# S5 state parts, sigmoids and latent-key scaling re-placed around two attention blocks

## The chip, the cores and the metric

One Trainium2 chip; the kernel runs on one core. The metric is the device time of one execution in microseconds (us), the median over runs. The engines are called PE (TensorE: matmuls and transposes), DVE (VectorE), ACT (ScalarE), POOL (GpSimd) and SP (SyncE, which here only issues DMAs). Each works through its own instructions in the order in which the program wrote them.

## The reference, cut to what matters

Two layers over 256 latent and 256 context tokens of width 1024. A layer is a half-step SwiGLU, a token mixer with three head groups side by side, and a second half-step SwiGLU. The change lies inside the mixer.

```
def token_mixers(zx, zc, need_ctx_out, ...):        # need_ctx_out: layer 0 only
    a_x = na_attention(rms_norm(heads(qa_x)), rms_norm(heads(ka_x)), va_x, ka_ch, va_ch, na_rpb)
    kb, vb = mla_keys_values(ckv, kr, ...)          # latent attention: low-rank keys and values
    qb_x = rope_tail(mla_queries(cq_x, ...), row, col)
    kb_x = rope_tail(kb_x, row, col)
    b_x = blocked_joint_attention(qb_x, kb_x, vb_x, kb_c, vb_c, MLA_QK ** -0.5)
    s_x, s_c = s5_mixer(u_x, u_c, ...)              # bidirectional complex scan, GELU, GLU
...
def mla_keys_values(ckv, kr, g_ckv, w_ukv, g_k):
    kv = (rms_norm(ckv, g_ckv) @ w_ukv).reshape(B, N, MLA_HEADS, MLA_NOPE + MLA_V_DIM)
    k = rms_norm(concatenate([k_nope, broadcast(kr)], axis=-1), g_k)
...
def readout(ys, u):
    a, g = split(gelu(ys[0] + ys[1] + d_skip * u) @ w_glu + b_glu, 2)
    return a * sigmoid(g)
```

## The kernel before, in words

The order of work is written out by hand: `tc.manual_schedule()` keeps the order of the Python code on every engine. Float32 products of the big projections are done as three matmuls (`mm3`, lines 291 to 293) on weights split into a high part (ACT, line 251) and a rest (line 252: DVE, and for the mixer's weights POOL for the second half); `take` splits the next weight unit ahead.

`mixers` handles one layer's token mixer in this order.

- Five projections by `group`: `cq`, `ckv`, `qa`, `ka`, `va`, each in two halves of weights. After every second `mm3`, `step` pops one entry of the list `self.q` or advances the background generator by one `yield`. The generator is `s5_mix`: in two half-groups (`hg`) it makes the scan of the S5 states on DVE (lines 1075, 1076), multiplies the real and the imaginary part back (`H[0]` and `H[1]`, lines 1084 to 1089) and multiplies both with the output matrices on PE (lines 1099, 1105, result `py`). The transposes of the window attention's queries and keys (`tr`) wait in `self.q` behind seven `None`.
- Up-projections of the latent attention: a list `seq` of token tiles, first the queries, then the four key tiles, each with a head (matmul and eviction), a stat (sum of squares and `rstd`, whose power runs on POOL, line 1140) and a tail. The queries' tail scales and rotates (`rope`); the keys' tail `ktail` scales the 64 plain columns on DVE (line 1359) and the 32 rotated ones on POOL (line 1360).
- The S5 gate: eight `mm3` (`wg`) into four PSUM banks `pg`, the six transposes of the latent queries into `mqT` (line 1123, evictions 1127 and 1131), the sum for the last key tile, the sigmoids (line 1387), the gate's product (line 1391) and its split (lines 1393, 1394).
- `attention`: 36 jobs in layer 0, 24 in layer 1, one per head and block of 128 queries, the window heads first. A job's scores (lines 1468 and 1473, or 1477) go to one of the four PSUM banks that `pg` also uses; maximum on DVE (1480), exponential on ACT (1484), scaling by 1/sum on DVE (1491) one turn later, transposes (1500) three turns later, products with the values (1520) after that. At turn 4 `k_cols` transposes all latent keys, 24 transposes, into `mkT`.

Of the kernel before, what the change touches and what calls it, by code (L numbers as in the profile page):

```python
# [10 lines left out]
F32 = mybir.dt.float32  # L11
F32R = mybir.dt.float32r
AF = mybir.ActivationFunctionType
OP = mybir.AluOpType
# [53 lines left out]
def bc(ap, shape):  # L68
    return ap.to_broadcast(shape)
# [24 lines left out]
class Net:  # L94
# [915 lines left out]
    def s5_mix(self, l, uT, yT):  # L1010
        nc = self.nc
        V, P, S = nc.vector, nc.gpsimd, nc.scalar
        with lines(self.tc, name=f"s5{l}", bufs=1, side="right") as sp:
            Ys = sp.tile([128, 8, 128], F32, name="Ys")
            for hg in range(2):
# [31 lines left out]
                for d in range(2):  # L1047
                    for pr in range(4):
                        for o in range(2):
                            for hf in range(2):  # L1050
# [3 lines left out]
                                q = (d * 4 + pr) * 64  # L1054
# [27 lines left out]
                for o, (x, y, op) in enumerate(((hr, hi, OP.subtract), (hi, hr, OP.add))):  # L1082
                    ua, ub = (ta, tb) if o == 0 else (tc2, td)
                    V.tensor_tensor(v4(ua), v4(x), Ec, op=OP.mult)
                    V.tensor_tensor(v4(ub), v4(y), Es, op=OP.mult)
                    a_, b_ = v4(ua), v4(ub)
                    V.tensor_tensor(H[o][:, 0, :, 1:64], a_[:, 0, :, 0:63], b_[:, 0, :, 0:63], op=op)
                    V.tensor_tensor(H[o][:, 1, :, 30::-1], a_[:, 1, :, 0:31], b_[:, 1, :, 0:31], op=op)
                    V.tensor_tensor(H[o][:, 1, :, 63:31:-1], a_[:, 1, :, 31:63], b_[:, 1, :, 31:63], op=op)
                    yield  # L1090
                for _ in range(4):
                    yield
                py = self.tp()
# [88 lines left out]
    def mixers(self, l, pu, nxt):  # L1182
        nc, I = self.nc, self.I
        V, P, S = nc.vector, nc.gpsimd, nc.scalar
        need = l == 0
        qt_ = [0, 1, 2, 3] if need else [2, 3]
# [3 lines left out]
        mp = pool(es, "mixa")  # L1190
        gb = mp.tile([128, 2, 32], F32, name="gb")
# [16 lines left out]
        def lowrank(z, n, kr=False):  # L1208
            def f(t):
                sq = np_.tile([128, 384], F32, name="sq")  # L1210
                ss = np_.tile([128, 1], F32, name="ss1", bufs=2)
                S.activation(sq[:, 0:n], z[:, t, 0:n], AF.Square, accum_out=ss)
                if kr:
                    S.activation(sq[:, 256:288], z[:, t, 256:288], AF.Square, accum_out=krs[:, t:t + 1])
                self.rstd(np_, ss, 1, n)
                V.tensor_scalar(z[:, t, 0:n], z[:, t, 0:n], ss, None, op0=OP.mult)

            return f
# [9 lines left out]
                    V.tensor_tensor(CG[:, i, 2 + t].rearrange("p (a b c) -> p a b c", a=2, b=2)[:, :, b, :],  # L1228
                                    kc[:, 2 + t].rearrange("p (a b c) -> p a b c", a=2, b=2)[:, :, b, :], g4[:, :, 1 - b, :], op=OP.mult)

        def rope(pl, x, t, i, nh):

            if t < 2:
                V.tensor_tensor(x, x, bc(gb[:, i, :].unsqueeze(1), [128, nh, 32]), op=OP.mult)
                return
            tm = pl.tile([128, nh, 32], F32, name="tm", bufs=2)
            q4 = lambda a: a.rearrange("p h (a b c) -> p h a b c", a=2, b=2)
            sg = CG[:, i, t].rearrange("p (a b c) -> p a b c", a=2, b=2)
            for b in range(2):
                for a in range(2):  # L1240
                    P.tensor_tensor(q4(tm)[:, :, a, b, :], q4(x)[:, :, a, 1 - b, :], bc(sg[:, a, b, :].unsqueeze(1), [128, nh, 8]), op=OP.mult)
            P.tensor_tensor(x, x, bc(CG[:, i, t - 2, :].unsqueeze(1), [128, nh, 32]), op=OP.mult)
            P.tensor_tensor(x, x, tm, op=OP.add)

        def kv(t):
            lowrank(zk, 256, True)(t)
            if t:
                rope(np_, zk[:, t - 1, 256:288].unsqueeze(1), t - 1, 1, 1)

        self.group("ckv", l, 288, al, lambda t: zk[:, t], kv)  # L1250
        rope(np_, zk[:, 3, 256:288].unsqueeze(1), 3, 1, 1)
        for qi, name in enumerate(("qa", "ka")):
            tiles = al if qi else qt_
            qn = np_.tile([128, 4, 384], F32, name="qn", bufs=2)

            def norm(t, qn=qn):
                sq = np_.tile([128, 384], F32, name="sq")
                S.activation(sq, qn[:, t], AF.Square)
                ss = np_.tile([128, 6], F32, name="ss", bufs=2)
                V.tensor_reduce(ss, sq.rearrange("p (h d) -> p h d", h=6), axis=AX, op=OP.add)  # L1260
                self.rstd(np_, ss, 6, 64)
                qv = qn[:, t].rearrange("p (h d) -> p h d", h=6)
                V.tensor_tensor(qv, qv, bc(ss.unsqueeze(2), [128, 6, 64]), op=OP.mult)

            self.group(name, l, 384, tiles, lambda t: qn[:, t], norm)

            def tr(j, qi=qi, tiles=tiles, qn=qn):
                self.transp(nq[qi][:, j, 128 * tiles[0]:], lambda t: qn[:, t, 128 * j:128 * j + 128], 128, tiles, self.kg[l][:, 0:1] if qi else None)

            self.q += [None] * 7 + [(lambda j=j, tr=tr: tr(j)) for j in range(3)]  # L1270
        self.group("va", l, 384, al, lambda t: nv[:, t])
        self.flush()

# [38 lines left out]
        qs, kn = {}, {}  # L1312
        new = lambda: lp.tile([128, 6, 96], F32, name="qn", bufs=4)

        ss = {}

        def stat(key, sq, extra=None):

            ss[key] = lp.tile([128, 6], F32, name="ss6", bufs=4)
            V.tensor_reduce(ss[key], sq, axis=AX, op=OP.add)  # L1320
            if extra is not None:
                V.tensor_scalar(ss[key], ss[key], extra, None, op0=OP.add)
            self.rstd(lp, ss[key], 6, 96)
# [33 lines left out]
        def ktail(t):  # L1357
            r = bc(ss["k", t].unsqueeze(2), [128, 6, 64])
            V.tensor_tensor(kn[t][:, :, 0:64], kn[t][:, :, 0:64], r, op=OP.mult)
            P.tensor_tensor(kn[t][:, :, 64:96], bc(zk[:, t, 256:288].unsqueeze(1), [128, 6, 32]), r[:, :, 0:32], op=OP.mult)  # L1360

        seq = [(qhead, qstat, qtail, t) for t in [2, 3] + qt_[:-2]]
        nqs = len(seq)
        seq += [(khead, kstat, ktail, t) for t in al]
        for i, s_ in enumerate(seq):
            if i == nqs:
                wk = self.take("ukv", (l,), True)[:, :, 0:1536].rearrange("p s (k n) -> p s k n", k=2)
            s_[0](s_[3])
            if i == nqs + 0:
                pass  # L1370
            for j in (1, 2):
                if i >= j:
                    seq[i - j][j](seq[i - j][3])
            if i - nqs - 1 in (0, 1):
                self.window(bias, i - nqs - 1)
# [4 lines left out]
            for k in range(2):  # L1380
                self.mm3(pg[n][:, c], (wg[:, 0, k, n * 128:n * 128 + 128], wg[:, 1, k, n * 128:n * 128 + 128]), (yh[:, 0, k, c], yh[:, 1, k, c]), k == 0, k == 1)
        eg = [zq.rearrange("p t n -> p (t n)")[:, T * n:T * n + T] for n in range(2)]
        for j in range(6):
            self.transp(mq[0][:, j, 128 * qt_[0]:], lambda t: qs[t][:, j, :], 96, qt_, eng="act" if j % 2 else "dve")
        seq[-1][1](seq[-1][3])
        for n in range(2):
            S.activation(eg[n][:, c], pg[2 + n][:, c], AF.Sigmoid, bias=self.smT[l][:, 98 + n:99 + n])
        seq[-2][2](seq[-2][3])
        seq[-1][2](seq[-1][3])
        for n in range(2):  # L1390
            V.scalar_tensor_tensor(eg[n][:, c], pg[n][:, c], self.smT[l][:, 96 + n:97 + n], eg[n][:, c], op0=OP.add, op1=OP.mult)
        for n in range(2):
            S.activation(xn[:, 0, 6 + n, c], eg[n][:, c], AF.Copy)
            (V,P)[n].tensor_tensor(xn[:, 1, 6 + n, c], eg[n][:, c], xn[:, 0, 6 + n, c].bitcast(F32), op=OP.subtract)
        esl.close()
        esr.close()

        def k_cols():
            for j in range(6):
                self.transp(mq[1][:, j, :], lambda t: kn[t][:, j, :], 96, al, self.kg[l][0:96, 1:2], eng="act" if j % 2 else "dve")  # L1400

        self.attention(l, need, nq, nv, mq, mv, bias, xn, k_cols)
# [38 lines left out]
    def attention(self, l, need, nq, nv, mq, mv, bias, ox, k_cols):  # L1441
        nc = self.nc
        V, P, S = nc.vector, nc.gpsimd, nc.scalar
        mm = nc.tensor.matmul
        with lines(self.tc, name=f"att{l}", bufs=1) as ap:
# [83 lines left out]
            for i in range(len(jobs) + LAG):  # L1529
                if i < len(jobs):  # L1530
                    scores(jobs[i])
                if 0 < i <= len(jobs):
                    scale(jobs[i - 1])
                if i >= LAG:
                    transposes(jobs[i - LAG])
                if i == 4:
                    k_cols()
                if i == 6:
                    self.ahead()
                for a in old.pop(0):  # L1540
                    pv(*a)
                old.append(pend[:])
                pend.clear()
# [48 lines left out]
```

## Time and profile before

| | us |
|---|---|
| median of 3 runs | 1966.84 (1964.74 to 1967.74) |
| the profiled execution, its own time | 1965.27 |
| its span, first to last instruction | 1963.5 |
| PE busy | 1906.2 (97%) |
| DVE, ACT, POOL busy | 912.7, 676.5, 559.3 |
| mean granted clock of PE, share of full speed | 0.983 |

PE is busy for 97% of the span, so time can only come out of its few waits and of stretches in which its clock is granted at half. The mixer's part before the feed-forward blocks lies at about 470 to 700 us (layer 0) and 1540 to 1745 us (layer 1).

### The profile page before, as it was taken

What the parts mean: (1) busy time and instruction counts of PE and PEld (TensorE: products, weight loads), DVE (VectorE), ACT (ScalarE), POOL (GpSimd) and SP (SyncE); (2) the same over time, 40 slices, a digit from 0 to 9 for tenths busy, and PEclk for the clock granted to TensorE, in tenths of its full rate; (3) what the DMA queues carried; (4) which work ended last, traced back from release to release, by engine and by line L of the source; (5) the groups of instructions that cost most, each with busy time, mean ns of one, the idle gap of its engine ahead of it and who ended that gap; (6) DMA issues with size and microseconds to landing.
All of it is one profiled execution on the core that took longest, in us unless ns stands there. A gap on an engine that the chain in (4) does not pass through costs nothing.

```text
span 1963.5 us, 28025 instructions
## 1 busy us (share of the span) xinstructions
PE 1906.2 (97%) x11345; PEld 1560.8 (79%) x11345; DVE 912.7 (46%) x1628; ACT 676.5 (34%) x1120; POOL 559.3 (28%) x637
## 2 busy tenths in 40 slices
PE   7999999999999999999999999999999888999999
PEld 4777777788895687788888877777888778579999
DVE  6453233247556835233232554423424745655555
ACT  4421222234444634212222342122223434545443
POOL 2137461124443032101101314745212435131000
PEclk9999999999997999999999999999999999799999
DMA  9656566524440024532322455646523443036563
GB/s 309 178 167 198 175 203 215 162 97 129 145 133 22 1 86 149 172 109 86 107 86 86 129 171 169 208 158 206 167 88 100 141 161 105 22 125 215 177 194 108
DMA packets 364101, 277.76 MB, mean 141 GB/s; under 512 B 29854, under 2 KB 355812, under 8 KB 363972
## 3 DMA queue, kind: packets, MB, share of 16 engines
q1 hardware_dynamic: 361008, 268.44, 43.8%
q0 software_dynamic: 1888, 7.31, 1.0%
q8 instruction: 89, 1.46, 0.3%
q10 hardware_dynamic: 1076, 0.22, 0.1%
q14 instruction: 40, 0.33, 0.1%
HBM read 263.39 MB, written 12.55 MB: 141 GB/s over the span
## 4 chain that ended last, share of the span: by engine, by line
PE 87%; DVE 5%; DMA 2%; POOL 2%; ACT 2%; issue 1%; SPq 1%; DVEq 0%; ACTq 0%; POOLq 0%
PE acc L291 25%; PE acc L292 24%; PE acc L293 24%; PE acc L1468 3%; PE b L467 3%; PE t L1500 1%; PE t L1520 1%; PE acc L1473 1%; DVE xm L562 1%; PE t L1105 1%; DVE xn L572 1%; PE acc L1477 1%; DVE spl L252 1%; POOL sqs L523 1%; PE t L1123 1%
## 5 line engine op out<-in xcount | busy, mean ns | idle before, releaser
L291 PE MATMUL acc<-xn,spl 128*128 128x512 f32 (+1 forms) x1664 | 597.1, 359 | 4.7 <-DVE mv L1348 2.7
L292 PE MATMUL acc<-xn,spl 128*128 128x512 f32 (+1 forms) x1664 | 590.2, 355 | 1.6 <-DVE xn L396 0.2
L293 PE MATMUL acc<-xn,spl 128*128 128x512 f32 (+1 forms) x1664 | 586.7, 353 | 0.1
L252 DVE TENSOR_TENSOR spl<-raw,spl 128x1024 fp32r<-128x1024 f32 (+2 forms) x312 | 393.2, 1296 | 274.4 <-ACT spl L251 272.3
L251 ACT ACTIVATE spl<-raw 128x1024 fp32r<-128x1024 f32 (+3 forms) x344 | 324.0, 990 | 307.5 <-PE acc L293 165.5
L291 PEld LDWEIGHTS acc<-xn,spl 128*128 128x128 f32 x1664 | 315.0, 189 | 67.3 <-issue 21.1
L292 PEld LDWEIGHTS acc<-xn,spl 128*128 128x128 f32 x1664 | 315.3, 189 | 46.5 <-DVE xn L570 4.0
L293 PEld LDWEIGHTS acc<-xn,spl 128*128 128x128 f32 x1664 | 315.1, 189 | 44.4 <-DVE spl L252 0.9
L672 POOL TENSOR_TENSOR hid<-hv,hid 128x512 fp32r<-128x512 f32 (+1 forms) x88 | 101.8, 1156 | 853.4 <-ACT hid L671 853.4
L291 PE MATMUL acc<-hid,spl 128*128 128x512 f32 (+1 forms) x740 | 265.2, 358 | 0.0
L292 PE MATMUL acc<-hid,spl 128*128 128x512 f32 (+1 forms) x740 | 262.0, 354 | 0.0
L293 PE MATMUL acc<-hid,spl 128*128 128x512 f32 (+1 forms) x740 | 261.8, 354 | 0.0
L669 DVE TENSOR_TENSOR hv<-sl,acc 128x512 f32<-128x512 f32 (+1 forms) x88 | 54.6, 621 | 360.1 <-PE acc L293 348.1
L729 DVE SCALAR_TENSOR_TENSOR h<-acc,mod,h 128x256 f32<-128x256 f32 x192 | 85.0, 479 | 210.3 <-PE acc L293 210.3
L671 ACT ACTIVATE hid<-hv 128x512 fp32r<-128x512 f32 (+1 forms) x88 | 50.9, 579 | 382.3 <-DVE hv L669 382.3
L291 PEld LDWEIGHTS acc<-hid,spl 128*128 128x128 f32 x740 | 139.8, 189 | 25.1 <-issue 6.4
L293 PEld LDWEIGHTS acc<-hid,spl 128*128 128x128 f32 x740 | 139.9, 189 | 19.7
L292 PEld LDWEIGHTS acc<-hid,spl 128*128 128x128 f32 x740 | 140.0, 189 | 18.6
L252 POOL TENSOR_TENSOR spl<-raw,spl 128x768 fp32r<-128x768 f32 (+3 forms) x32 | 65.0, 2030 | 214.4 <-ACT spl L251 204.0
L291 PE MATMUL acc<-spl,xn 128*128 128x384 f32 (+1 forms) x322 | 108.7, 338 | 0.0
L292 PE MATMUL acc<-spl,xn 128*128 128x384 f32 (+1 forms) x322 | 105.1, 326 | 1.1 <-DVE spl L252 1.1
L293 PE MATMUL acc<-spl,xn 128*128 128x384 f32 (+1 forms) x322 | 104.6, 325 | 0.0
(360 smaller groups left out, 1993.4 us busy)
## 6 DMA issues: line engine op xcount, KB each, us to landing
raw<-in_ffn_w_gu SPq DMA_DIRECT2D x176, 512.0 KB
raw<-in_w_mod SPq DMA_DIRECT2D x64, 1024.0 KB
raw<-in_ffn_w_down SPq DMA_DIRECT2D x32, 1024.0 KB
raw<-in_ffn_w_down SPq DMA_DIRECT2D x16, 768.0 KB
raw<-in_w_in SPq DMA_DIRECT2D x16, 768.0 KB
pmod<-in_w_mod SPq DMA_DIRECT2D x8, 1024.0 KB
raw<-in_w_out SPq DMA_DIRECT2D x8, 1024.0 KB
cld<-CL POOLq DMA_DIRECT2D x8, 576.0 KB, 4.1
```

What stands on the lines that cost most here:

```text
L251: nc.scalar.activation(s[:, 0, a:b], raw[:, a:b], AF.Copy)
L252: (nc.gpsimd if mix and b == n else nc.vector).tensor_tensor(s[:, 1, a:b], raw[:, a:b], s[:, 0, a:b].bitcast(F32), op=OP.subtract)
L291: mm(out, sl[0], sr[0], start=start, stop=False)
L292: mm(out, sl[0], sr[1], start=False, stop=False)
L293: mm(out, sl[1], sr[0], start=False, stop=stop)
L467: nc.tensor.matmul(p[32 * j:32 * j + 32, 0:256], self.cs[:, k, 6 - 2 * w:38 - 2 * w], raw[:, k, :], start=(a == 0 and w == 0), stop=(a == ...
L523: nc.gpsimd.tensor_tensor(self.sq_sum[:, c], self.sq_sum[:, c], s[:, c], op=OP.add)
L669: nc.vector.tensor_tensor(hv[:, c], sl[:, c], pu[:, c], op=OP.mult)
L671: nc.scalar.activation(hd[:, 0, c], hv[:, c], AF.Copy)
L672: nc.gpsimd.tensor_tensor(hd[:, 1, c], hv[:, c], hd[:, 0, c].bitcast(F32), op=OP.subtract)
L729: self.nc.vector.scalar_tensor_tensor(self.h[:, n, c], ps[:, c], self.mod[l][:, gate, n, s:s + 1], self.h[:, n, c], op0=OP.mult, op1=OP.add)
L1468: mm(s, q[:, 256 + 128 * t:384 + 128 * t], k, start=True, stop=h >= 6)
```

## The change

Four edits.

1. In `s5_mix` both parts `H[0]` and `H[1]` are made in one turn of the generator. Before, one turn lay between them; five turns pass behind the second part as before, so the second part and the products `py` stand one turn, that is two `mm3`, earlier.
2. `rope` for the shared rotated key columns writes into a tile of its own, `kr`, and its four small POOL products become two of twice the width.
3. The transposes of the window queries and keys wait behind nine `None` instead of seven.
4. In front of the attention: the keys' tails leave the list; the sigmoids stand before the query transposes, of which three come before and three after the gate's product; the four `ktail` go into turns 2 to 5 of the attention, the key transposes into turns 6 and 7 (twelve each), and `self.ahead()` (the split of the next weights) from turn 6 to turn 8. The keys' sums get a tile `ssk` that outlives the pool.

```diff
                     V.tensor_tensor(H[o][:, 1, :, 63:31:-1], ...)
-                    yield
-                for _ in range(4):
+                for _ in range(5):
                     yield
...
+        kr = mp.tile([128, 4, 32], F32, name="kr")
+        def rope(pl, x, t, i, nh, to=None):
+            to = x if to is None else to
...
             for b in range(2):
-                for a in range(2):
-                    P.tensor_tensor(q4(tm)[:, :, a, b, :], q4(x)[:, :, a, 1 - b, :], bc(sg[:, a, b, :]...), op=OP.mult)
+                P.tensor_tensor(q4(tm)[:, :, :, b, :], q4(x)[:, :, :, 1 - b, :], bc(sg[:, :, b, :]...), op=OP.mult)
...
-            self.q += [None] * 7 + [(lambda j=j, tr=tr: tr(j)) for j in range(3)]
+            self.q += [None] * 9 + [(lambda j=j, tr=tr: tr(j)) for j in range(3)]
...
-                if i >= j:
+                if i >= j and (j == 1 or i - j < nqs):
                     seq[i - j][j](seq[i - j][3])
...
-        for j in range(6):
-            self.transp(mq[0][:, j, ...], ..., 96, qt_, eng="act" if j % 2 else "dve")
         seq[-1][1](seq[-1][3])
         for n in range(2):
             S.activation(eg[n][:, c], pg[2 + n][:, c], AF.Sigmoid, ...)
-        seq[-2][2](seq[-2][3])
-        seq[-1][2](seq[-1][3])
+        for j in range(3):
+            self.transp(mq[0][:, j, ...], ..., 96, qt_, eng="act" if j == 2 else "dve")
...
+        for j in range(3, 6):
+            self.transp(mq[0][:, j, ...], ..., 96, qt_, eng="act" if j % 2 else "dve")
...
-        def k_cols():
-            for j in range(6):
+        def k_cols(n):
+            if n < 4:
+                ktail(n)
+                return
+            for j in range(3 * n - 12, 3 * n - 9):
...
-                if i == 4:
-                    k_cols()
-                if i == 6:
+                if 1 < i < 8:
+                    k_cols(i - 2)
+                if i == 8:
                     self.ahead()
```

On DVE in layer 1, second half-group of the S5 part, before: the last product of the real part, the norms of two query tiles (`qn`), the split of the next weights (line 252), and then the imaginary part (the second `H`).

```order
L1089 TENSOR_TENSOR H_12574<-ab 128x4x32
L1156 COPY qn<-acc 128x384
L1260 TENSOR_REDUCE ss<-sq 128x6
L1139 TENSOR_SCALAR ss<-ss 128x6
L1263 TENSOR_TENSOR qn<-qn,ss 128x384
...
L252 TENSOR_TENSOR spl<-raw,spl 128x768
L1084 TENSOR_TENSOR ab<-si,E 128x512
L1085 TENSOR_TENSOR ab<-sr,E 128x512
L1087 TENSOR_TENSOR H_12575<-ab 128x4x63
```

The same place in the change, from the four products in front of the scan (`ab`) on; one split (line 252) now stands behind those products instead of before them.

```order
L1067 TENSOR_TENSOR ab<-t,E 128x512
L252 TENSOR_TENSOR spl<-raw,spl 128x768
...
L1089 TENSOR_TENSOR H_12555<-ab 128x4x32
L1084 TENSOR_TENSOR ab<-si,E 128x512
L1085 TENSOR_TENSOR ab<-sr,E 128x512
L1087 TENSOR_TENSOR H_12556<-ab 128x4x63
...
L1155 COPY qn<-acc 128x384
L1261 TENSOR_REDUCE ss<-sq 128x6
```

The second part has moved in front of both norms and of the split that followed them.

On ACT in layer 1, ahead of the attention, before: the evictions of three query transposes, the squares of the last key tile, the load of the sigmoid's table and the sigmoids (into `zq`).

```order
L1127 ACTIVATE mqT<-b 96x256
L1127 ACTIVATE mqT<-t 96x256
L1127 ACTIVATE mqT<-b 96x256
L1354 ACTIVATE sq_13266<-kn 128x6x64
L1387 ACT_TABLE_LOAD
L1387 ACTIVATE zq<-acc,smT_91 128x256 x2
L1393 ACTIVATE xn<-zq 128x256 x2
```

And in the change:

```order
L1356 ACTIVATE sq_13219<-kn 128x6x64
L1387 ACT_TABLE_LOAD
L1387 ACTIVATE zq<-acc,smT_91 128x256 x2
L1126 ACTIVATE mqT<-t 96x256
L1393 ACTIVATE xn<-zq 128x256 x2
L1126 ACTIVATE mqT<-t 96x256
L1126 ACTIVATE mqT<-b 96x256
```

The sigmoids no longer stand behind any eviction of a transpose.

On DVE at the same place of layer 1, before: the sums and powers of the last two key tiles, their scalings (line 1359), and between them the evictions of three query transposes.

```order
L1359 TENSOR_TENSOR kn<-kn,ss_13141 128x6x64
L1348 COPY kn<-acc 128x3x64
L1348 COPY mv<-acc 128x192
...
L1359 TENSOR_TENSOR kn<-kn,ss_13176 128x6x64
L1131 COPY mqT<-t 96x256 x3
...
L1359 TENSOR_TENSOR kn<-kn,ss_13205 128x6x64
L1359 TENSOR_TENSOR kn<-kn,ss_13268 128x6x64
L1391 SCALAR_TENSOR_TENSOR zq<-acc,smT_91,zq 128x256 x2
```

And in the change:

```order
L1350 COPY kn<-acc 128x3x64
L1350 COPY mv<-acc 128x192
...
L1138 TENSOR_SCALAR ssk<-ssk 128x6
L1130 COPY mqT<-t 96x256
L1130 COPY mqT<-b 96x256
L1391 SCALAR_TENSOR_TENSOR zq<-acc,smT_91,zq 128x256 x2
L1394 TENSOR_TENSOR xn<-zq,xn 128x256
L1130 COPY mqT<-t 96x256
```

No scaling of keys, which waits for a power on POOL, is left in front of the evictions; the four scalings follow within the first attention jobs.

## Rows read from the trace of the kernel before

**Rows 1.** Stretches around layer 0's first attention jobs; columns in the first line.

```profile
core 0: us, PE busy (x) PEld busy (x) DVE busy (x) ACT busy (x) POOL busy (x), PEclk, DMA share, GB/s
599.00:604.00 5.00, 2.66 (x4) 0.99 (x4) 3.40 (x7) 3.27 (x5) 2.82 (x3) 0.70 0.00 0
614.00:619.00 5.00, 5.00 (x20) 3.76 (x19) 3.29 (x8) 2.28 (x7) 0.00 (x0) 0.50 0.00 0
619.00:624.00 5.00, 5.00 (x28) 4.15 (x27) 2.63 (x4) 2.05 (x3) 0.00 (x0) 0.76 0.00 0
634.00:639.00 5.00, 5.00 (x28) 3.02 (x27) 4.54 (x12) 2.76 (x10) 0.00 (x0) 1.00 0.42 147
```

**Rows 2.** Stretches of layer 1's mixer, the same columns.

```profile
1632.00:1636.00 4.00, 2.60 (x15) 2.31 (x16) 2.91 (x3) 2.60 (x4) 0.77 (x2) 1.00 0.16 43
1664.00:1668.00 4.00, 1.10 (x5) 0.65 (x4) 1.95 (x4) 0.86 (x3) 4.00 (x5) 0.74 0.00 0
1688.00:1692.00 4.00, 4.00 (x25) 3.36 (x23) 2.90 (x5) 2.29 (x5) 0.00 (x0) 0.77 0.00 0
```

**Rows 3.** PE's waits in layer 0's mixer: total us, times, longest us.

```profile
PE acc L1468 <- ACT zq L1387: 3.1, 1, 3.1
PE acc L291 <- DVE mv L1348: 1.5, 1, 1.5
PE t L1105 <- DVE H L1087: 1.3, 1, 1.3
PE b L1123 <- DVE qn L1263: 1.0, 1, 1.0
PE acc L292 <- DVE spl L252: 0.7, 2, 0.4
```

**Rows 4.** PE's waits in layer 1's mixer, the same columns.

```profile
PE t L1105 <- DVE H L1087: 7.0, 1, 7.0
...
PE acc L1468 <- ACT zq L1387: 2.7, 1, 2.7
PE t L1123 <- DVE mqT L1131: 2.4, 1, 2.4
...
PE acc L291 <- DVE mv L1348: 1.2, 1, 1.2
```

**Rows 5.** Chain in order of time, layer 1: start, us, what.

```profile
1670.14 2.07 PE acc L1468 x2
...
1691.40 1.05 PE acc L1468 x2
...
1734.14 1.91 PE b L1520 x14
```

**Rows 6.** Timeline of layer 1's second S5 half-group: start, us, what, [idle before].

```profile
1588.57 0.96 DVE L252 TENSOR_TENSOR spl<-raw,spl 128x768 fp32r<-128x768 f32 x1 [5.48 <-ACT spl L251]
...
1597.78 2.03 PE L1105 MATMUL t<-C,H 64*64 64x128 f32 x32
...
1605.29 0.94 DVE L252 TENSOR_TENSOR spl<-raw,spl 128x768 fp32r<-128x768 f32 x1
...
1608.04 3.54 PE L1105 MATMUL t<-C,H 64*64 64x128 f32 x32 [6.96 <-DVE H L1087]
```

**Rows 7.** Timeline in front of layer 0's first scores, the same columns.

```profile
592.77 0.55 DVE L1359 TENSOR_TENSOR kn<-kn,ss 128x384 f32<-128x384 f32 x1
...
597.64 0.60 PE L1123 MATMUL b<-k,qn 128*96 128x128 f32 x4
...
599.30 1.28 ACT L1387 ACT_TABLE_LOAD   x1
...
601.34 1.22 PE L1468 MATMUL acc<-nkT,nqT 64*128 64x512 f32 x1 [3.09 <-ACT zq L1387]
```

**Rows 8.** POOL's rotation of layer 1's last query tile, the same columns.

```profile
1660.30 1.32 POOL L1241 TENSOR_TENSOR tm<-qn,CG 128x48 f32<-128x48 f32 x4
...
1662.38 0.60 POOL L1243 TENSOR_TENSOR qn<-qn,tm 128x192 f32<-128x192 f32 x1
```

More of the change, by code (lines that the diff above doesn't have):

```diff
@@ L1229, in mixers @@
                                     kc[:, 2 + t].rearrange("p (a b c) -> p a b c", a=2, b=2)[:, :, b, :], g4[:, :, 1 - b, :], op=OP.mult)
-        def rope(pl, x, t, i, nh):
+        kr = mp.tile([128, 4, 32], F32, name="kr")
+        def rope(pl, x, t, i, nh, to=None):
+            to = x if to is None else to
             if t < 2:
-                V.tensor_tensor(x, x, bc(gb[:, i, :].unsqueeze(1), [128, nh, 32]), op=OP.mult)
+                V.tensor_tensor(to, x, bc(gb[:, i, :].unsqueeze(1), [128, nh, 32]), op=OP.mult)
                 return
@@ L1239, in rope @@
             for b in range(2):
-                for a in range(2):
-                    P.tensor_tensor(q4(tm)[:, :, a, b, :], q4(x)[:, :, a, 1 - b, :], bc(sg[:, a, b, :].unsqueeze(1), [128, nh, 8]), op=OP.mult)
+                P.tensor_tensor(q4(tm)[:, :, :, b, :], q4(x)[:, :, :, 1 - b, :], bc(sg[:, :, b, :].unsqueeze(1), [128, nh, 2, 8]), op=OP.mult)
             P.tensor_tensor(x, x, bc(CG[:, i, t - 2, :].unsqueeze(1), [128, nh, 32]), op=OP.mult)
-            P.tensor_tensor(x, x, tm, op=OP.add)
+            P.tensor_tensor(to, x, tm, op=OP.add)
         def kv(t):
@@ L1247, in kv @@
             if t:
-                rope(np_, zk[:, t - 1, 256:288].unsqueeze(1), t - 1, 1, 1)
+                rope(np_, zk[:, t - 1, 256:288].unsqueeze(1), t - 1, 1, 1, kr[:, t - 1].unsqueeze(1))
         self.group("ckv", l, 288, al, lambda t: zk[:, t], kv)
-        rope(np_, zk[:, 3, 256:288].unsqueeze(1), 3, 1, 1)
+        rope(np_, zk[:, 3, 256:288].unsqueeze(1), 3, 1, 1, kr[:, 3].unsqueeze(1))
         for qi, name in enumerate(("qa", "ka")):
@@ L1315, in mixers @@
         ss = {}
+        ssk = knp.tile([128, 4, 6], F32, name="ssk")
         def stat(key, sq, extra=None):
-            ss[key] = lp.tile([128, 6], F32, name="ss6", bufs=4)
+            ss[key] = lp.tile([128, 6], F32, name="ss6", bufs=2) if key[0] == "q" else ssk[:, key[1]]
             V.tensor_reduce(ss[key], sq, axis=AX, op=OP.add)
@@ L1359, in ktail @@
             V.tensor_tensor(kn[t][:, :, 0:64], kn[t][:, :, 0:64], r, op=OP.mult)
-            P.tensor_tensor(kn[t][:, :, 64:96], bc(zk[:, t, 256:288].unsqueeze(1), [128, 6, 32]), r[:, :, 0:32], op=OP.mult)
+            P.tensor_tensor(kn[t][:, :, 64:96], bc(kr[:, t].unsqueeze(1), [128, 6, 32]), r[:, :, 0:32], op=OP.mult)
         seq = [(qhead, qstat, qtail, t) for t in [2, 3] + qt_[:-2]]
@@ L1382, in mixers @@
         eg = [zq.rearrange("p t n -> p (t n)")[:, T * n:T * n + T] for n in range(2)]
-        for j in range(6):
-            self.transp(mq[0][:, j, 128 * qt_[0]:], lambda t: qs[t][:, j, :], 96, qt_, eng="act" if j % 2 else "dve")
         seq[-1][1](seq[-1][3])
@@ L1387, in mixers @@
             S.activation(eg[n][:, c], pg[2 + n][:, c], AF.Sigmoid, bias=self.smT[l][:, 98 + n:99 + n])
-        seq[-2][2](seq[-2][3])
-        seq[-1][2](seq[-1][3])
+        for j in range(3):
+            self.transp(mq[0][:, j, 128 * qt_[0]:], lambda t: qs[t][:, j, :], 96, qt_, eng="act" if j == 2 else "dve")
         for n in range(2):
@@ L1394, in mixers @@
             (V,P)[n].tensor_tensor(xn[:, 1, 6 + n, c], eg[n][:, c], xn[:, 0, 6 + n, c].bitcast(F32), op=OP.subtract)
+        for j in range(3, 6):
+            self.transp(mq[0][:, j, 128 * qt_[0]:], lambda t: qs[t][:, j, :], 96, qt_, eng="act" if j % 2 else "dve")
         esl.close()
         esr.close()
-        def k_cols():
-            for j in range(6):
+        def k_cols(n):
[3 more added lines that the diff above has]
+            for j in range(3 * n - 12, 3 * n - 9):
                 self.transp(mq[1][:, j, :], lambda t: kn[t][:, j, :], 96, al, self.kg[l][0:96, 1:2], eng="act" if j % 2 else "dve")
```

## The prediction

> **What bounds the kernel now.** The page comes first: PE is busy for 97% of the span, so the question is what its other 3% are and what its clock does. So I read the stretches with their granted clock next. In layer 0 the clock falls at about 601 us (the stretch of 599 to 604 has a mean of 0.70, which is 2 us at full and 3 at half), is 0.50, the lower of its two levels, through 614 to 619, and comes back in 619 to 624 at about 621.4 (0.76 is 2.4 us of half) [rows 1]. In layer 1 it falls within 1664 to 1668, when PE was busy for 1.10 of 4 us, and comes back at about 1689.8 (0.77 in 1688 to 1692 is 1.8 us of half) [rows 2]. That is 20 us at half speed in each layer, while PE works without a gap on the first attention jobs. Then the waits of PE: in layer 0 the longest is the first scores on a sigmoid, 3.1 us, then the gate on a copy of values, 1.5 [rows 3]; in layer 1 the S5 product on the second `H`, 7.0, then the first scores on a sigmoid, 2.7, the query transposes on an eviction, 2.4, and the gate on a copy, 1.2 [rows 4]. The reader is to see that the waits in front of the attention are small, and that what they bring, a clock at half for the next 20 us, is worth more than they are. The price is in the chain: the same pair of scores takes 2.07 us at 1670 and 1.05 at 1691 [rows 5].
>
> **Layer 0, up to the first scores.** Today ACT loads the sigmoid's table at 599.30, behind three evictions and the squares of the last key tile; PE has finished its last transposes at 598.2 (597.64 and 0.60) and waits until 601.34 [rows 7]. In the change ACT has no eviction in front, and the squares need only DVE's third key sum, which no scaling delays. I put both sigmoids at about 596.5 and the scores' start at 597.2, so all 3.1 go. Of the gate's 1.5 about 1.0 goes: the copy stood behind one scaling of 0.55 [rows 7], and POOL, on whose powers DVE waits there, saves some 0.45 for a rotated tile: its four narrow products take 1.32, 0.33 each, and 0.60 is paid for an operation four times as wide [rows 8], so two of double width should take 0.40 to 0.45 each (an estimate between those two rows). Together 4.1; bounds 3.1 and 4.6.
>
> **Layer 0, the clock.** If PE keeps full speed, 20.1 us at half shrink by 1.05/2.07 [rows 5] to 10.2. This saves 9.9; bounds 9.0 and 10.2.
>
> **Layer 1, up to the first scores.** The waits of 2.7, 2.4 and 1.2 have one root each in rows that move: evictions stand behind scalings that wait for powers on POOL, the sigmoid behind evictions, the value copy behind a scaling. They come to 6.3. What is late next is POOL's rotation of the last query tile: it ends at 1662.98 [rows 8], with two rotations shortened perhaps at 1662.1, while PE is there 1.2 earlier than now, so a wait of some 0.6 stays at the transposes. POOL has also still to make three powers before its half of the gate's split, and the first maximum on DVE reuses memory that this split reads; the jobs run three turns ahead of their transposes, so I charge only that and a little more: 6.2 in place of 6.3, since the transposes behind the waits then also run at full speed. Bounds 5.3 and 7.2.
>
> **Layer 1, the clock.** From 1670.1 to 1689.8 at half, 19.7 us, saves 9.7 by the same ratio [rows 2, 5]; bounds 9.0 and 9.9.
>
> **Layer 1, the S5 parts.** PE's products with the first part run at 1597.78 and take 2.03; those with the second wait 6.96 and take 3.54, since the clock has fallen meanwhile [rows 6]. DVE, which had the second part's inputs since the scan, did two norms and a split (to 1606.2) first. In the change the second part follows the first, so 7.0 and 1.5 go. Behind it now stand the norms and the split of the next key weights, which PE needs after six more `mm3`. They come up to 2 us later (1606.2 to 1608.0 is the second part's time up to PE's start) and up to 2.9 earlier, because the four products ahead of the scan no longer stand behind a split that waited 5.48 for ACT [rows 6]. PE gets there at about 1605 (an estimate: two products of 2.03 and some 4 us for eight `mm3`, started a good microsecond earlier than now), the split is ready between 1603 and 1608.3; I take a new wait of 1.5. Gain 7.0; bounds 5.0 and 8.5. In layer 1's first half-group the second part follows the first already, and nothing is gained; two `mm3` that now stand behind the products make PE arrive a little earlier and wait that much longer, which the later wait gives back.
>
> **The rest.** Layer 0's S5 wait of 1.3 [rows 3] goes as well, but the split behind it comes later: 0.6, bounds 0 and 1.3. The two further `None` gain nothing where it looks as if they should: the wait of 1.0 for a norm is followed by one for the split (half of the 0.7) [rows 3], and the split stands behind that norm on DVE. PE then meets the split instead, without the transposes to fill about 0.45 of it: minus 0.7, bounds minus 1.4 and 0. The key scalings cost DVE 4 times 0.55 within four jobs. In layer 0 at full clock DVE is busy for 4.54 of 5 us [rows 1], so not all of it fits: minus 1.0 for both layers, bounds minus 2.0 and 0. The later split of the output weights is hidden by the rest of the attention; were it not, it would cost at most its DVE part, by the 0.96 for 768 columns [rows 6] about 1.3 us. The wider POOL products and the tile `kr` change only what is said above.
>
> **Sum.** 4.1 + 9.9 + 6.2 + 9.7 + 7.0 + 0.6 - 0.7 - 1.0 = 35.8 us off the profiled execution's own 1965.27: 1929.5. The median of the runs is 1.6 above that execution, so 1931. With all lower bounds 28 us go (1939), with all upper ones 42 (1925).
>
> **Will the clock stay up?** More than half of the sum hangs on this. In layer 1 between 1632 and 1636 PE was busy for only 2.60 of 4 us and the clock stayed at 1.00; it fell where PE had 1.10 of 4 [rows 2]. The change leaves, between the gate's last matmul and the first scores, transposes and waits of well under 1 us in each layer. Transposes themselves seem to hold the clock: it came back in both layers just when PE ran the 24 key transposes, and not in the scores before them [rows 1, 2].
>
> The Trainium skill, page "TensorE: Matmul & The Clock Gate", section "Part 4: PE-mode transpose", says the opposite, that transposes do not count as a busy PE for the clock. By it the 2.7 us of transposes in layer 0 and about 2 us in layer 1 would be as good as idle and the next rival would be the likeliest, at 1945 or 1959. The rows just named do not agree with it.
>
> **Rivals.** One: the clock falls in one layer all the same, with a somewhat longer wait than I reckon. Then half speed lasts until the key transposes, which now stand at turns 6 and 7 and not at 4: the 9.8 are lost, and two more jobs run at half, about 2 us each (a job's first pair alone costs 1.02 more [rows 5]). 14 us less gain: 1945; in both layers 1959. For it: the clock fell after waits of 3.1 and 2.4 us. Against: the waits that did this are the ones that go.
>
> Two, on the other side: the clock falls in one layer and the key transposes, now two lots of 12 instead of one of 24, are too short to bring it back. Then the rest of that attention runs at half. In layer 1 it lasts from 1691.4 to 1736.0 [rows 5], 44.6 us, which would cost as much again: 1931 + 9.7 + 44.6 = 1985. This decides as soon as half speed goes on for more than about 26 us of work behind the key transposes in one layer. For it: today the scores alone did not bring the clock back. Against: it must fall first.
>
> Three: the S5 gain is given back at the key weights' split, and with it the clock falls there again: 5 us less, 1936, inside the likeliest case's range.
>
> Four: the waits only move (first maxima behind POOL's late split, PE stopping at turn 3), and the clock goes with them in both layers, with no S5 gain: about 1966, no change.
>
> **How the numbers follow.** The likeliest, clock up in both layers, 0.73, with 1925 to 1939 of its own; one layer down 0.13 (1945); both down 0.05 (1959); no change 0.03; slower 0.06 (1985). Within 0.2%, 4 us, is what a measurement of this kernel cannot tell from no change. So faster 0.91, same 0.03, slower 0.06. The range runs from 1924 to 1948: the likeliest case and the fall in one layer, with one microsecond at either end.
>
> **What the profile after would show.** The wait of the first scores on the sigmoid gone in both layers, scores starting about 3 us after the gate's last matmul; a granted clock of 1.00 through the first attention jobs, a pair of scores at 1.05 from the first; in layer 1 no wait on `H` in the second half-group but one of 0 to 3 us on line 252; the wait for the norm in front of the window transposes replaced by one on line 252 of about the same length. I would be wrong if the clock row shows 0.50 behind the gate, or if PE waits in turns 3 to 8 on DVE's line 1491 or on evictions of keys for more than 2 us in a layer.

## The result, and the profile after

The changed kernel takes 1937.5 us (median of 4 runs, 1935.6 to 1937.9) against 1966.6 before: a ratio of 0.985, 95% interval 0.983 to 0.987, 29 us less. (Ratios here and below are against runs of the kernel before on the same chip.) Its profiled execution has a span of 1936.0, 27.5 under that of before.

The traces are compared by stages between instants of PE: the first S5 transposes (of `UC`), the first latent transposes (of `zq`), the first scores and the end of the last value product of each layer, and in layer 1 also the first transposes of the second S5 half-group. After, layer 0's stand here (timeline: start, us, what):

```profile
468.64 0.71 PE L1041 MATMUL b<-k,UC 64*128 64x64 f32 x8
571.53 1.04 PE L1122 MATMUL t<-k,zq 128*128 128x128 f32 x8
601.03 1.12 PE L1474 MATMUL acc<-nkT,nqT 64*128 64x512 f32 x2
681.91 1.24 PE L1526 MATMUL t<-PTc,mv 128*64 128x256 f32 x8
```

The same instants of every trace give this table (us). S5: S5 beside the low-rank and window groups, in layer 1 its first (a) and second (b) half-group and what follows it; lat: latent products and gate; att: attention.

| kernel | median | S5, 0 | lat, 0 | att, 0 | S5a, 1 | S5b, 1 | lat, 1 | att, 1 |
|---|---|---|---|---|---|---|---|---|
| before | 1966.6 | 100.8 | 33.9 | 90.9 | 32.9 | 63.6 | 27.1 | 65.9 |
| after | 1937.5 | 102.9 | 29.5 | 82.1 | 34.2 | 57.8 | 20.6 | 58.4 |
| fill_mm | 1956.0 | 100.8 | 35.0 | 82.3 | 33.9 | 64.2 | 29.8 | 57.1 |
| fill_tr | 1951.2 | 100.8 | 33.9 | 83.5 | 34.0 | 63.8 | 26.6 | 57.1 |
| keys_late | 1961.9 | 103.0 | 32.7 | 91.0 | 33.8 | 57.9 | 23.2 | 69.3 |
| keys_front | 1949.4 | 102.9 | 30.1 | 84.1 | 32.5 | 57.9 | 24.7 | 65.4 |
| none7 | 1935.4 | 99.9 | 29.5 | 82.1 | 33.5 | 59.9 | 20.6 | 58.4 |
| none9_only | 1969.5 | 102.3 | 33.9 | 90.8 | 32.9 | 63.6 | 27.0 | 65.9 |
| s5_apart | 1944.3 | 102.4 | 29.5 | 82.1 | 33.1 | 63.8 | 20.6 | 58.4 |
| s5_only | 1960.1 | 99.9 | 33.9 | 91.1 | 33.2 | 60.3 | 27.1 | 66.0 |
| s5_y6 | 1941.8 | 102.8 | 29.5 | 82.1 | 34.0 | 64.4 | 20.6 | 58.4 |
| no_key_scale | 1933.3 | 102.9 | 29.5 | 81.4 | 33.2 | 59.5 | 20.6 | 57.4 |
| late_products | 1927.5 | 99.9 | 29.5 | 82.1 | 39.8 | 46.6 | 20.6 | 58.4 |
| late_scan | 1926.1 | 99.8 | 29.5 | 82.1 | 42.4 | 43.1 | 20.6 | 58.4 |

Stages that an edit leaves alone mostly agree to 0.2 us. The first half-group does not (32.5 to 34.2 in the twelve kernels that keep its order), nor does the second in no_key_scale (59.5, where after has 57.8 with the same code there; see the two `None` below), nor what lies ahead of layer 0's first instant (465.5 to 469.4 us in all fourteen). The stages are therefore the finer measure: after minus before they give +2.1 - 4.4 - 8.7 + 1.2 - 5.7 - 6.5 - 7.5 = -29.5. The two spans differ by 2 less, because after's first instant came 2.0 later.

The stretches of after (columns as in [rows 1]; the first four of layer 0, the others of layer 1):

```profile
540.00:542.00 2.00, 2.00 (x9) 2.00 (x8) 2.00 (x1) 0.00 (x0) 1.28 (x1) 0.56 0.56 97
542.00:544.00 2.00, 2.00 (x10) 1.91 (x9) 0.10 (x1) 0.11 (x1) 0.00 (x0) 0.58 1.03 392
599.00:604.00 5.00, 5.00 (x27) 2.97 (x25) 4.25 (x7) 4.80 (x9) 3.73 (x4) 1.00 0.02 3
614.00:619.00 5.00, 4.44 (x30) 3.32 (x29) 4.93 (x12) 2.84 (x9) 0.00 (x0) 1.00 0.00 0
...
1560.00:1564.00 4.00, 4.00 (x30) 3.39 (x28) 1.59 (x4) 0.18 (x1) 0.00 (x0) 0.50 0.00 0
...
1648.00:1652.00 4.00, 3.35 (x16) 1.81 (x17) 2.88 (x8) 3.34 (x9) 3.99 (x5) 1.00 0.00 0
...
1664.00:1668.00 4.00, 3.20 (x20) 2.04 (x19) 3.93 (x10) 2.62 (x6) 0.00 (x0) 1.00 0.01 4
```

Behind both gates the clock is 1.00, where the kernel before had fallen to 0.50 [rows 1, 2]. In the two mixers two falls are left: a new one of 3.4 us from 540 in layer 0's groups, and one of 6.8 from 1557 in layer 1's first S5 half-group (3.4 before); the 6.8 that before has from 1604, at its wait on the second `H`, are gone. In the first attention jobs DVE is now busy for 4.93 of 5 and 3.93 of 4 us. PE's waits, layer 0 and then layer 1, are these:

```profile
PE acc L292 <- DVE spl L252: 4.2, 2, 2.4
PE t L1122 <- DVE kn L1361: 0.6, 1, 0.6
...
PE acc L291 <- DVE mv L1350: 0.2, 1, 0.2
...
PE t L1104 <- POOL rg L1027: 6.0, 1, 6.0
PE acc L292 <- DVE spl L252: 2.4, 2, 2.2
PE acc L292 <- POOL H L1081: 1.4, 1, 1.4
PE t L1122 <- POOL qn L1244: 0.9, 1, 0.9
PE t L1122 <- DVE kn L1361: 0.8, 1, 0.8
```

Of [rows 3, 4] the sigmoid, the eviction and the second `H` are gone. Instead PE waits on splits (line 252; the 1.4 put down to `H` too, since POOL had just ended its half of a split there).

### The profile page after: what moved, and what is told of

It is laid out like the page before. It is cut to its first block, busy times and chain, and to the rows that moved or that the text cites. A ratio compares the mean times of both kernels' runs of the same rounds, so it can differ in the third digit from the quotient of the medians.

```text
span 1936.0 us, 28006 instructions
## 1 busy us (share of the span) xinstructions
PE 1888.9 (98%) x11345; PEld 1552.8 (80%) x11345; DVE 916.2 (47%) x1628; ACT 675.9 (35%) x1120; POOL 558.4 (29%) x621
## 4 chain that ended last, share of the span: by engine, by line
PE 85%; DVE 7%; POOL 3%; ACT 1%; DMA 1%; issue 1%; SPq 0%; POOLq 0%; DVEq 0%; ACTq 0%
PE acc L291 25%; PE acc L292 24%; PE acc L293 24%; PE b L467 3%; PE acc L1474 2%; POOL ss L1139 1%; DVE xm L562 1%; PE t L1526 1%; PE t L1104 1%; PE t L1506 1%; DVE xn L572 1%; POOL sqs L523 1%; DVE spl L252 1%; PE t L1122 1%; DVE xn L570 1%
## 5 line engine op out<-in xcount | busy, mean ns | idle before, releaser
L293 PEld LDWEIGHTS acc<-hid,spl 128*128 128x128 f32 x740 | 139.9, 189 | 19.7
```

The source lines that it names most:

```text
L293: mm(out, sl[1], sr[0], start=False, stop=stop)
```

## Experiments

**Is it the clock?** Before, with work for PE that nobody reads, ahead of the fifth query transpose of layer 1 and of both layers' first scores; in fill_tr each `matmul` is transposes of the same width.

```
+            if j == 3 and not need:
+                busy(pj[:, 256:512], 8, 256)
+        busy(self.tp(), 5, 512)
```

> The kernel before, unchanged but for matmuls whose results nobody reads, put where PE waits today: eight of 256 columns in front of the fifth query transpose of layer 1 (a wait of 2.4 us) and five of 512 in front of the first scores of both layers (waits of 3.1 and 2.7). The waits stay, PE is busy in them. Theory (the clock is more than half of the gain, and only idleness in front of the scores takes it away): the clock stays at 1.00 through the first attention jobs of both layers, and 15 to 20 us go, 1947 to 1952. Rival (the slow first jobs come from what ACT, DVE and POOL have to do there, or the clock falls for another reason): 1965 to 1970.

> The same with transposes against the identity (16 and 20 of 128 columns) in place of the matmuls. Theory (transposes hold the clock as matmuls do, as the rows of the key transposes suggested): as with matmuls, 1947 to 1953. Rival (the rule of the Trainium skill, page TensorE: Matmul & The Clock Gate, section Part 4: PE-mode transpose, that transposes do not count): the clock falls as before, 1965 to 1969.

Measured: 1956.0, a ratio of 0.994 (0.993 to 0.996), and 1951.2, 0.993 (0.991 to 0.994). The clock is 1.00 behind both gates in both. The attention stages are 8.5 and 8.9 us shorter with matmuls, 7.4 and 8.8 with transposes, and this with nothing made ready any earlier than before. The matmuls gave part of it back: they take 4.46 us in front of the scores, where 3.1 and 2.7 were idle. So the theory holds: of the change's 29.5 us some 16, the 8.7 and 7.5 of its attention stages, are the clock. Layer 1 of fill_tr, timeline and stretch:

```profile
1660.42 2.35 PE L1386 MATMUL t<-k,nkT 128*128 128x128 f32 x20
1663.25 1.12 PE L1476 MATMUL acc<-nkT,nqT 64*128 64x512 f32 x2 [0.48 <-ACT zq L1395]
...
1660.00:1664.00 4.00, 3.52 (x27) 2.82 (x26) 2.06 (x6) 2.92 (x5) 3.50 (x4) 1.00 0.00 0
```

PE has run transposes alone since 1656, and the first pair of scores takes 1.12, not 2.07 [rows 5]. The Trainium skill's sentence on this (page "TensorE: Matmul & The Clock Gate", section "Part 4: PE-mode transpose", that full clock does not engage for transposes, which do not count as a busy PE in the same way) does not hold here.

**Which edit keeps it up?** The changed kernel with one of the two edits undone: in keys_late the sigmoids behind the transposes, in keys_front the key scalings in front of the attention (and with them the key transposes in one lot at turn 4 and `ahead` at turn 6, as before).

```
keys_late:
+        for j in range(6):
+            self.transp(mq[0][:, j, 128 * qt_[0]:], ...)
         for n in range(2):
             S.activation(eg[n][:, c], pg[2 + n][:, c], AF.Sigmoid, ...)
-        for j in range(3):
...
keys_front:
-                if i >= j and (j == 1 or i - j < nqs):
+                if i >= j:
...
-                if 1 < i < 8:
-                    k_cols(i - 2)
+                if i == 4:
+                    k_cols()
```

> The changed kernel with the sigmoids behind the query transposes and their evictions again; the key scalings stay within the attention jobs. Theory (ACT's three evictions in front of the sigmoid are enough for a wait that costs the clock): the first scores wait 2 to 3 us on the sigmoid in both layers, the clock falls behind it in both, the stages of the attention take 90 and 66 us as before: 1955 to 1960. Rival (the key scalings and the powers they wait for were what made the sigmoid late): waits under 1 us, clock at 1.00, 1937 to 1940.

> The changed kernel with the key scalings in front of the attention and the key transposes in the fourth turn again; the sigmoids stay in front of the query transposes. Theory (by the waits of before: gate on the value copy 1.5 and 1.2, layer 1's transposes on an eviction 2.4, come back, since copies and evictions stand behind scalings; the scores' wait on the sigmoid does not): 2 to 5 us slower, 1940 to 1943, clock at 1.00 in layer 0, and in layer 1 too unless the 2.4 comes back whole; with its clock lost there, 1948 to 1952. The wait of 0.6 to 0.8 on a scaled key in the attention (2.0 us in all with what else stands behind DVE there) goes in return. Rival (the sigmoids' place is the whole matter): 1935 to 1938.

Measured: keys_late 1961.9, ratio 0.999 (0.998 to 1.000); keys_front 1949.4, 0.992 (0.991 to 0.994). PE's waits, the first two of keys_late, the third of keys_front in layer 1, and two stretches of keys_front behind the gates of layer 0 and layer 1:

```profile
PE acc L1472 <- ACT zq L1389: 3.1, 1, 3.1
...
PE acc L1472 <- ACT zq L1389: 2.7, 1, 2.7
...
PE t L1122 <- DVE mqT L1130: 3.3, 1, 3.3
...
603.00:607.00 4.00, 3.55 (x9) 1.18 (x8) 2.86 (x5) 3.94 (x8) 2.98 (x4) 1.00 0.00 0
1656.00:1660.00 4.00, 4.00 (x7) 1.36 (x6) 2.45 (x6) 3.41 (x7) 3.05 (x5) 0.50 0.00 0
```

With the sigmoids behind the evictions both waits are exactly those of before, and the clock falls in both layers; with the scalings in front it falls in layer 1 alone, behind an eviction. So for the clock layer 0 needs one edit and layer 1 both. (Layer 0's attention is 2.0 us longer in keys_front all the same, at full clock: PE waits up to 1.6 there on an exponential that DVE scales by 1/sum.) Where the clock comes back, keys_late's timeline shows in layer 1:

```profile
1683.99 2.07 PE L1472 MATMUL acc<-nkT,nqT 64*128 64x512 f32 x2
1687.86 2.28 PE L1122 MATMUL t<-k,kn 128*96 128x128 f32 x12
1690.07 1.12 PE L1472 MATMUL acc<-nkT,nqT 64*128 64x512 f32 x2
```

The first lot of 12 key transposes is enough. That strikes out rival two, and PE had been busy without a gap in the jobs ahead of it, scores with at most four transposes each. Moving the key transposes moved the clock's return with them: it lies 22 us (layer 0) and 27 us (layer 1) behind the first scores here, 20 in both layers before, and within the key transposes each time.

**What the two None cost.** Seven in the changed kernel (none7), nine in the one before (none9_only).

```
-            self.q += [None] * 9 + [...]
+            self.q += [None] * 7 + [...]
```

> The changed kernel with seven None in place of nine. The trace after shows waits of 4.2 us (layer 0) and 2.4 us (layer 1) on the split at line 252 behind the norm groups, where before had 2.5 and 2.0 in three pieces. Theory A (the two further None cost them: PE meets the split without the transposes that filled part of it): 1 to 3 us faster than the change, 1934 to 1937. Theory B (the second S5 part on DVE, in front of the split, costs them): within 1 us of the change, 1937 to 1939, with the waits back on the norm.

> The kernel before with nine None and nothing else of the change. By the prediction's term (minus 0.7, bounds minus 1.4 and 0): 1966 to 1968.5. By what seven None gave in the changed kernel (3.0 us lost in layer 0, 1.3 gained in layer 1): the stage of layer 0 from S5 to the latent transposes 2 to 3 us longer with a wait of about 4 us on the split in two pieces and a dip of the clock behind one of them, layer 1's 1 us shorter, 1967 to 1969. Rival (the loss in layer 0 needs the second S5 part in front of the split too): no more than 0.5 us lost in layer 0.

Measured: none7 1935.4, 0.984 (0.982 to 0.985), an interval that overlaps the change's; none9_only 1969.5, 1.002 (1.001 to 1.003). In the stages nine None cost layer 0 1.5 us alone and 3.0 within the change; in layer 1 they cost nothing alone and gain 2.1 within it, 1.7 of that because a fall of 3.4 us at half, behind a wait of 1.9 on a norm in none7, is not there. But this 1.7 can't be put down to the None: no_key_scale has nine too, and the same wait on a split, and there the clock does fall (PE and a stretch of after, then of no_key_scale):

```profile
1619.94 0.45 PE L292 MATMUL acc<-spl,xn 128*128 128x384 f32 x1 [2.19 <-DVE spl L252]
1620.00:1624.00 4.00, 4.00 (x26) 3.92 (x27) 2.71 (x1) 1.07 (x2) 1.79 (x1) 1.00 0.40 109
...
1617.70 0.44 PE L292 MATMUL acc<-spl,xn 128*128 128x384 f32 x1 [2.19 <-DVE spl L252]
1618.00:1622.00 4.00, 4.00 (x17) 3.90 (x16) 2.45 (x1) 0.32 (x1) 1.54 (x1) 0.59 0.45 118
```

That leaves 0.4 for the None in layer 1. Theory A holds for layer 0. What is behind layer 0's wait (DVE, POOL and PE of after):

```profile
556.09 0.56 DVE L1264 TENSOR_TENSOR qn<-qn,ss 128x384 f32<-128x384 f32 x1 [1.50 <-POOL ss L1139]
...
558.82 2.16 DVE L1264 TENSOR_TENSOR qn<-qn,ss 128x384 f32<-128x384 f32 x1 [1.50 <-POOL ss L1139]
560.90 3.77 DVE L252 TENSOR_TENSOR spl<-raw,spl 128x768 fp32r<-128x768 f32 x2
...
558.75 1.81 POOL L252 TENSOR_TENSOR spl<-raw,spl 128x768 fp32r<-128x768 f32 x1
...
561.90 0.44 PE L292 MATMUL acc<-spl,xn 128*128 128x384 f32 x1 [2.40 <-DVE spl L252]
```

The last norm and POOL's half of the split start together, the norm takes 2.16 in place of 0.56, and DVE's half of the split comes behind it. With seven None transposes fill part of that; with nine PE idles at once, 4.2 us in two waits, and in the change the clock fell behind one of them (3.4 us at half cost 1.7). So it did in all five traces with nine None and both S5 parts in one turn, behind the first wait in two and behind the second in three; in none9_only and s5_apart it did not, with 4.4 in two waits. Why is left open.

**What the S5 edit is worth.** Taken out of the change (s5_apart), put alone into before (s5_only), and with the products a step later (s5_y6).

```
s5_apart, in the loop over o:
+                    yield
-                for _ in range(5):
+                for _ in range(4):
s5_y6:
-                for _ in range(5):
+                for _ in range(6):
```

> The changed kernel with the two S5 parts in two turns again. Prediction's own sizes: the wait of 7.0 on H comes back in layer 1 with the half clock behind it, less the new split waits: 6 to 8 us slower than the change, 1943 to 1946. Rival (the S5 gain is mostly given back at the split, since the trace after shows layer 1's S5 and group stage only 4.5 us shorter and layer 0's 2 us longer): 1938 to 1941.

> The kernel before with both S5 parts in one turn and nothing else of the change. By the prediction's term (7.0 in layer 1, 0.6 in layer 0): 1957 to 1960. By what taking it out of the changed kernel gave in the stages (4.8 us gained in layer 1, 0.5 lost in layer 0): 1961 to 1964, with the wait on the second H gone in the second half-group and the first half-group's wait 1.2 us longer, with half clock for 7 to 8 us behind it in place of 3 to 4.

> The changed kernel with six idle turns behind the two S5 parts in place of five, so that the products stand where they stood before. Theory (the first half-group of layer 1 lost 1.2 us of wait and some 4 us more at half clock because the products came a step earlier): the wait of 6.0 is 4.8 again, the half clock behind it 3 to 4 us in place of 7.8, 2 to 4 us faster than the change. Rival (how long half clock lasts there has nothing to do with the step): within 1.2 us of the change.

Measured: s5_apart 1944.3, 0.989 (0.987 to 0.990); s5_only 1960.1, 0.998 (0.996 to 0.999); s5_y6 1941.8, 0.988 (0.986 to 0.989). The second half-group gains 5.9 us by the edit within the change and 3.3 alone (with seven None the clock falls behind the next norm, as in none7; against no_key_scale, where it falls too, the gain within the change is 4.3); layer 0 gains 1.0 alone and loses 0.5 within the change, where the new fall counts against it. In the first half-group PE's wait is longer with the edit, 6.0 in five of six kernels (4.7 in keys_front) and 4.8 in all six without it or with its step undone, but the stage is not: it takes 32.5 to 34.2 in the former and 32.9 to 34.0 in the latter, so the 34.2 of after lies at the end of a scatter. (The 7 to 8 us at half in two expectations are 6.8.) s5_y6, 4.3 us slower than the change, bore out neither of its theories. The wait is 4.8 again, the half clock is not shorter, and the second half-group loses the whole gain. PE's waits in its layer 1:

```profile
PE acc L292 <- DVE spl L252: 7.5, 2, 4.8
PE t L1104 <- issue: 4.8, 1, 4.8
```

With the products a step later the last S5 transposes stand behind the next split and not ahead of it, PE meets that split 4.8 us early, and the clock falls. So the order on DVE alone gains nothing here: the gain needs the saved step too.

**What the key scalings cost.** The change without DVE's four scalings of a layer (the unrotated columns of the latent keys stay unscaled).

```
-            V.tensor_tensor(kn[t][:, :, 0:64], kn[t][:, :, 0:64], r, op=OP.mult)
```

> The changed kernel without DVE's four scalings of the latent keys in each layer (the 64 unrotated columns of each head stay unscaled), to price them within the attention jobs. Theory (DVE sets the pace of the first jobs at full clock): the waits of the key transposes on a scaled key (0.6 and 0.8 us) and of a transpose on an exponential (0.6) go, 1 to 2 us less in all, most of it in layer 1. Rival (the jobs wait on something else, POOL's half of the split or ACT): the two attention stages stay at 82.1 and 58.4 us.

Measured: 1933.3, 0.984 (0.982 to 0.985). The attention stages are 0.75 and 0.97 shorter: 1.7 us. The waits on a scaled key are gone, those on an exponential stay (0.6 in layer 1), so the theory holds in part.

**A faster one.** Seven None in layer 0, nine in layer 1, and the products of layer 1's first half-group later (late_products), or its scans and S5 parts later (late_scan, shown). In the other half-groups late_products has six turns in front of the products, as s5_y6, and late_scan five:

```
-                yield
-                yield
+                for _ in range(8 if l and not hg else 2):
+                    yield
...
-                yield
+                for _ in range(5 if l and not hg else 1):
+                    yield
...
-            self.q += [None] * 9 + [...]
+            self.q += [None] * (7 if need else 9) + [...]
```

> Meant to beat both: the changed kernel with seven None in layer 0 and nine in layer 1, and the products of layer 1's first half-group eight steps further behind its scan, so that PE has low-rank matmuls in place of the wait of 6.0 us. Theory (that wait and the half clock behind it are PE arriving too early at the end of a DVE chain): wait and half clock of that half-group go, 6 plus 3 to 4 us, and 3 us in layer 0's groups: 8 to 12 us faster than the change, 1926 to 1930. Rival (the chain only moves: the second half-group follows later and waits as long, or runs into the end of the value group): 1933 to 1938.

> Meant to beat the last one too: seven None in layer 0, nine in layer 1; in layer 1's first half-group the scans stand six steps later (behind DVE's half of the next split) and the two S5 parts another four steps behind them. Theory (what is left there, a wait of 4.2 us on the split and 2.6 us at half clock, is DVE doing scans and S5 parts in front of a split whose input it has had since 1547): that wait is under 2 us and the clock stays up, 2 to 5 us faster than with the products alone put later, 1922 to 1926. Rival (DVE has the same work to do between the same two points, so the wait only moves on to the next split or to the products): 1926 to 1930.

Measured: 1927.5, 0.981 (0.980 to 0.983), and 1926.1, 0.980 (0.978 to 0.981): both beat the change, by 8.6 and 9.6 us in the stages, 3.0 of it in layer 0. The first lies in its theory's range, and the wait of 6.0 is gone, but in its place PE waits 4.2 on a split and the clock falls there for 3.4 us in place of 6.8; in the second half-group both waits on a split are gone (one of 1.4 on an eviction by ACT is new). The second adds nothing that the intervals tell: its wait moved on, as the rival had it. PE waits for the split again, and the clock falls there for 6.8 us (waits in layer 1's first half-group, late_products and then late_scan):

```profile
PE acc L292 <- DVE spl L252: 4.2, 1, 4.2
...
PE acc L292 <- POOL spl L252: 2.5, 1, 2.5
PE acc L292 <- DVE spl L252: 1.2, 1, 1.2
```

## Why the prediction was right, term by term

The time (1931 forecast, range 1924 to 1948) was right in sign, in its likeliest case and in the mechanism of its largest terms, and 6.5 us too fast. Its sum was 35.8, the stages give 29.5.

| term | predicted | measured | from |
|---|---|---|---|
| waits up to the first scores, layers 0 and 1 | 4.1, 6.2 | 4.4, 6.5 | lat stages, after and before |
| clock, both layers | 19.6 | 18.0 | att stages, no_key_scale and before |
| key scalings | -1.0 | -1.7 | att stages, after and no_key_scale |
| S5, layers 1 and 0 | 7.0, 0.6 | 5.9 (alone 3.3), -0.5 (alone 1.0) | S5b and S5 stages, s5_apart and after, s5_only and before |
| nine None | -0.7 | layer 0 -3.0 (alone -1.5), layer 1 +2.1 (alone 0.0) | S5 and S5b stages, none7 and after, none9_only and before |
| S5 and None together | 6.9 | 3.7 | -2.1 in S5, 0 and +5.7 in S5b, 1, before and after |
| first half-group, layer 1 | 0 | -1.2 | scatter |

- **Waits in front of the scores.** Right, in place and cause. Layer 0's stage begins 4.1 us later in after's trace; with that taken off, the sigmoids end at 596.2 and the first scores start at 597.0 (596.5 and 597.2 forecast). Layer 1's new wait on POOL's rotation is 0.9 (0.6 forecast), though two wide products take 0.74 where four narrow ones took 1.32, a saving of 0.58 (0.45 forecast). No run undoes this edit alone, so what it is worth in time is not shown.
- **The clock.** Right, and shown apart from the waits by the fillers. Its size was taken as the whole half-speed stretch by the ratio of [rows 5]. Of the 1.6 that are missing, 0.6 is a new wait on an exponential in layer 1, where DVE is late at full clock. The rest comes out by the ratio. The 1.05 is a row of the chain, which leaves out what overlaps with the matmul ahead. From one pair's start to the next it is 3.15 at half and 1.68 at full (before, then fill_tr):

```profile
604.49 2.07 PE L1468 MATMUL acc<-nkT,nqT 64*128 64x512 f32 x2
607.64 2.07 PE L1468 MATMUL acc<-nkT,nqT 64*128 64x512 f32 x2
...
601.48 1.12 PE L1476 MATMUL acc<-nkT,nqT 64*128 64x512 f32 x2 [0.91 <-ACT zq L1395]
603.16 1.12 PE L1476 MATMUL acc<-nkT,nqT 64*128 64x512 f32 x2
```

At 1.68/3.15 the forecast's 20.1 and 19.7 us would have saved 9.4 and 9.2, 1.0 less. Measured are 9.5 and 8.5, the second with that wait of 0.6 in it.

- **Key transposes hold and bring back the clock.** Read from [rows 1, 2] alone; shown by fill_tr and keys_late.
- **S5.** Right in place, forecast too large: 5.9 in layer 1, inside the bounds (5.0 to 8.5), but 4.3 when the clock falls behind the next split as in no_key_scale. The new wait on the split behind the products is 0.3 (1.5 forecast), and one of 1.4 on a split stands ahead of them. The first half-group gained nothing, and PE's wait there grew from 4.8 to 6.0, both as forecast; the 1.2 that after's trace loses there is scatter.
- **None.** The step that failed ("PE then meets the split instead", priced at 0.7), and with S5 the largest miss: 3.2 of the 6.3. The sign was right, but layer 0's -3.0 is far beyond the bound of -1.4 for both layers. The forecast counted the transposes that no longer fill the wait (0.45), and saw neither that the last norm takes 2.16 beside POOL's split (before's own trace has it, 2.17 at 555.20), nor that the clock can fall behind such a wait. That both layers together come to -0.9, near the forecast, is luck: layer 1's gain was not foreseen and is mostly a fall that came or stayed away.
- **Key scalings.** 1.7 for 1.0, inside their bound of 2.0, and by the cause named: DVE.
- **Rivals.** One (1945 or 1959) did not come, but keys_front and keys_late stand near it, with the clock down in one layer and in both: 1949 and 1962. Two is struck out. Three came in part: splits take back some of the S5 gain, but the clock does not fall there in after. That its 1936 lies so near the 1937.5 measured is luck, since half of the miss lies in other terms.

## What to carry to other kernels

Look at the granted clock behind each wait of PE: here waits of 2.4 to 3.3 us in front of the attention cost another 7 to 11 behind them, and work that nobody reads, put into the gap, brought 11 to 16 us by itself. Not every such wait does: one of 2.19 cost the clock in one trace and not in another. When a wait is taken away, follow the two engines that shared it to the next thing they owe PE; here it was a split, three times. And put an edit that loses in one layer under a condition that keeps it to the other.

## What the runs showed of the hardware

Transposes against the identity, put in place of waits of 3.1 and 2.7 us, kept the clock at 1.00 where those waits had taken it away, and 12 in a row brought it back where scores with at most four transposes a job, PE busy without a gap, had not.

An elementwise product on DVE of two tiles in SBUF took 0.56 alone and 2.16 when POOL had begun a subtraction of 1.81 just ahead of it; it ended 0.4 after POOL's end at 560.56. The subtraction lost nothing: with DVE idle beside it, it takes 1.84 (after):

```profile
518.98 1.84 POOL L252 TENSOR_TENSOR spl<-raw,spl 128x768 fp32r<-128x768 f32 x1
```

So DVE stood still for most of it, and the two did not share. The Trainium skill says so (page "SBUF — State Buffer", section "SBUF: two separate sides": whichever of DVE and GpSimd starts first holds their common port pair for the whole instruction, and the other is blocked, if the DVE operation has two inputs in SBUF and the GpSimd one reads SBUF); the rows agree.
